# Hybrid decoder layer: two query heads take x's first k tile beside the first projection, and single-block attention products become fp32 matmuls

## The chip, the cores and the metric

The kernel runs on one core of a Trainium2 chip. The metric is device time in microseconds (us) of one launch; smaller is better. The engines are named as in the profile: PE multiplies matrices (PEld loads its weights), DVE and ACT work on vectors, POOL fills constants and issues some DMAs, SP issues most DMAs.

## What is computed

One decoder layer over 512 tokens of width 1024, all in float32:

```python
h = rms_norm(x, g_mix)
q, f, i, gate, mq, mk, mv = split(h @ W_in)      # HGRN2: 4 x 512 columns; MoBA: 3 x 512
f  = lb + (1 - lb) * sigmoid(f);  k = 1 - f;  b = cumsum over 32 tokens of log(f)
A  = causal((q * exp(b)) @ (k * exp(-b)).T)       # per head, in chunks of 32
o  = A @ i + (q * exp(b)) @ S;   S = decay * S + (k * exp(b_last - b)).T @ i
o  = rms_norm_per_head(o) * silu(gate)
m  = causal softmax attention of mq, mk (partial rotary), mv, 4 heads of 128
x  = x + concat(o, m) @ W_out
x  = x + cross_attention(rms_norm(x), mem)        # 256 memory tokens
x  = x + relu(rms_norm(x) @ W1) ** 2 @ W2         # width 4096
out = rms_norm(x)
```

With 512 tokens in two blocks of 256 and the own block always taken, the block choice of the MoBA heads is plain causal attention.

## The kernel before, in words

**Products of three.** Almost every large product is written as three fp32r matmuls: each operand is split into a rounded part (`hi`, written by ACT) and the rest (`lo`, a subtraction on DVE), and hi*hi, hi*lo and lo*hi are added in PSUM. Weights come in units of 128x1024 (512 KB): SP loads a unit into one of three raw buffers (`wr4` for unit 4), ACT writes `wh4`, DVE writes `wl4`. A raw buffer is free for the load three units on when its `wl` is written. `need(u)`, called as a stage begins to use unit u, asks for loads six units ahead and splits two ahead (`load_unit`, `split_unit`).

**Stages.** They follow each other on PE: `hf` (forget logits, units 0 to 3, all four heads side by side, k tile by k tile of x), `hi` (the recurrence's input, units 4 to 7, token-major, `tm_stage`), `hq` (queries, units 8 to 11, one head after the other, `fm_stage`), `mv`, `mkq`, `hg`, then the output projection `wo`, cross-attention, the MLP and the last norm. Each takes 24 matmuls of 128x512 for one unit. The norm's factor is not applied to x ahead of the products, but to their results: `norm_rows` sums x's squares (`nr`, two matmuls during `hf`), then `rsqrt_of` makes the root by Ln and Exp on ACT (`rb1`).

**The recurrence.** `ev_f` multiplies `hf` by the root, takes the sigmoid on ACT and the lower bound on DVE, all into `Fz`. One Ln over all four heads gives `lnf`. `hgrn_pre(h)` makes the running sums `b` (a scan on DVE), the exponentials `eb`, `kt` and `Fz` on ACT and some twenty small DVE steps (`dc`, `ee`, `pp`, `ss`, `ke`). `ev_q` takes a head's finished `hq` and writes `qx0`, `qx1` (two halves of the tokens) and `q4` on DVE. `hgrn_out(h)` transposes `ke` (`ket`), multiplies `qx` with `kt` and `Fz` on PE (`a`, 28 small matmuls), and goes on to `pd`, the state `S` and the output `ho`.

**Attention.** `moba_head` makes the scores in four blocks of queries (`sc`: block s has (s+1) times 128 keys), the softmax, transposes the probabilities (`pt`) into `PT` and their low parts into `PL` and unused corners of `PT`, and multiplies by the values `Vm`, `Vml` (`po`).

**Order.** The start, up to the last k tile of `hf`, is kept in the order in which it is written (`ordered`). From there a scheduler sets the order on each engine from the dependencies and its own costs, and the small steps of `hgrn_pre`, `hgrn_out` and `moba_head` are put between the large matmuls by `pump` when a planner (`Pace`) takes their operands to be ready. Each engine then runs its list strictly in order. Sums of later weights are made in memory by DMAs that POOL issues (`m`, `u`), on a queue of their own, in marked places of PE's list.

**Start.** SP loads x's first k tile (256 KB); ACT's own queue loads the first k tile of unit 0 in two pieces of 128 KB (heads 0 and 1, heads 2 and 3). PE meanwhile runs `warm`, products of ones that nobody reads.

Of the kernel before, what the change touches and what calls it, by code (L numbers as in the profile page):

```python
# [8 lines left out]
F32 = mybir.dt.float32  # L9
F32R = mybir.dt.float32r  # L10
# [5 lines left out]
P = 128  # L16
D = 1024
T = 512
# [107 lines left out]
def hybrid_layer(ctx: ExitStack, tc: tile.TileContext, xT, memT, ws, vecs, consts, rots, out):  # L126
# [40 lines left out]
    def acc_bank(name):  # L167
        return pacc.tile([P, T], F32, tag="acc", name=name)
# [130 lines left out]

    transfers = all_sums()  # L300
    AFTER = mybir.DependencyInfo(mybir.DependencyClass.Sync, mybir.DependencyReason.DATA)
    marks = [None]

    def more_sums():
# [25 lines left out]
            return line[u - W_WO][0] in ("wo", "xo")  # L330
        return u % 2 == 0 and (4 <= u - FF2 < 14 or u - FF2 >= 26)

    held = []

    def later(f):
        held[0].append(f) if held else f()

    def split_raw(u, raw, a, b, eng=None):
        A.activation(his[u][:, a:b], raw[:, a:b], AF.Copy)

        def lower(hi=his[u], lo=los[u]):
            (eng or V).tensor_sub(lo[:, a:b], raw[:, a:b], hi[:, a:b].bitcast(F32))
        later(lower)
# [57 lines left out]
        if s == 2:  # L401
            more_sums()

    def need(u):
        marks.append(last_mm[0])
        if MLP <= u + SPLIT_AHEAD < FF2:
            f1_prep(*divmod(u + SPLIT_AHEAD - MLP, 7))
            return
        last = MLP if u < MLP else UNITS
        most = RAWS if u < MLP else 2 * RAWS  # L410
        want_load, want_split = min(last, u + LOAD_AHEAD + 1), min(last, u + SPLIT_AHEAD + 1)
        while state["split"] < want_split or state["load"] < want_load:
            if state["load"] < want_load and state["load"] - state["split"] < most:
                load_unit()
            elif state["split"] < want_split:
                split_unit()
            else:
                break
        if MLP - 6 <= u < MLP - 2:
            for what in ("A", "B", "cC", "D")[u - MLP + 6]:  # L420
                f1_load(0, what)
        if MLP - 7 <= u < MLP - 2:
            more_sums()
# [3 lines left out]

    side = []
    made = {}
    GAP, SLACK, WARM = 4, 2.5, 11  # L430
    since = [0]
    last_mm = [None]

# [81 lines left out]
                        between(u + j)  # L515
            u += size

    def tm_stage(u0, act, ntok, evac, name):

        accs = [acc_bank(f"{name}{t}") for t in range(ntok)]  # L520
        for j in range(4):
            need(u0 + j)
            hi, lo = his[u0 + j], los[u0 + j]
            for t in range(ntok):
                for kk in range(2):
                    a_hi, a_lo = act(2 * j + kk)
                    a_hi, a_lo = a_hi[:, t * P:(t + 1) * P], a_lo[:, t * P:(t + 1) * P]
                    w_hi, w_lo = hi[:, kk * T:(kk + 1) * T], lo[:, kk * T:(kk + 1) * T]
                    st = j == 0 and kk == 0
                    mm(accs[t], a_hi, w_hi, st, False)  # L530
                    mm(accs[t], a_hi, w_lo, False, False)
                    mm(accs[t], a_lo, w_hi, False, j == 3 and kk == 1)
                if j == 3:
                    evac(t, accs[t])
# [38 lines left out]
    def split_first(v, k, h=slice(None)):  # L573
        hi, lo, raw = (by_k(t)[:, h, k] for t in (his[v], los[v], raws[v]))
        A.activation(hi, raw, AF.Copy)
        V.tensor_sub(lo, raw, hi.bitcast(F32))

    SY.dma_start(vec, vecs)
    load_x(0)
    load_first(0, 0, slice(0, 2), A)  # L580
    load_first(0, 0, slice(2, 4), A)
    load_x(1)
    load_first(0, 1)
    load_x(2)
# [56 lines left out]
    A.activation(x0h[:, :T // 2], x0r[:, :T // 2], AF.Copy, scale=gain(G_MIX, 0))  # L641
    V.scalar_tensor_tensor(x0l, x0r, gain(G_MIX, 0), x0h.bitcast(F32), op0=ALU.mult, op1=ALU.subtract)
    split_first(0, 0, slice(2, 4))
    split_x(1)
    split_first(0, 1)
    load_first(3)
# [22 lines left out]
    def rsqrt_of(dst, src, div):  # L669

        A.activation(dst, src, AF.Ln, bias=eps, scale=1.0 / div)
        A.activation(dst, dst, AF.Exp, scale=-0.5)

    def column_sums(ps, src, n, name, later=None):

# [47 lines left out]


    accs = [(acc_bank if j < 2 else side_bank)(f"hf{j}") for j in range(HEADS)]
    norm_x = norm_rows(Sx, T, rb1, rc1)
    next(norm_x)
    for k in range(KT):
        if k % 2 == 0:
            need(k // 2)  # L730
        if k == KT - 1:
            next(norm_x)
            lower_bounds()
            ordered.__exit__(None, None, None)
        a_hi, a_lo = x_act(k)
        for hs in ((0, 1), (2, 3)) if k in (0, 2) else ((0,), (1,), (2,), (3,)):
            w = {h: [by_k(t[k // 2])[:, h, k % 2] for t in (his, los)] for h in hs}
            for h in hs:
                mm(accs[h], w[h][0], a_hi, k == 0, False)
            for h in hs:  # L740
                mm(accs[h], w[h][1], a_hi, False, False)
            for h in hs:
                mm(accs[h], w[h][0], a_lo, False, k == KT - 1)
    for h in range(HEADS):
        ev_f(h, accs[h])
    start(norm_x, "nx", 1.0)
    u = 4
# [100 lines left out]
        drain("nx")  # L848
        A.activation(Vh[:, t, :], acc, AF.Copy, scale=rc1[:, t:t + 1])

    tm_stage(u, x_act, 4, ev_hi, "hi")
    u += 4

    def ev_q(h, acc):
# [17 lines left out]
                         H["pp"][:, t0:t0 + 2, :, None].to_broadcast([P, 2, 4, CHUNK]))  # L872
        start(hgrn_out(h, qx, q4), ("out", h))

    fm_stage(u, x_act, T, ev_q, "hq", ONE * 4)
    u += 4


    Vm, Vml = s8(F32R, "Vm"), s8(F32R, "Vml")

    def ev_mv(t, acc):
        A.activation(Vm[:, t, :], acc, AF.Copy, scale=rc1[:, t:t + 1])
        V.scalar_tensor_tensor(Vml[:, t, :], acc, rc1[:, t:t + 1], Vm[:, t, :].bitcast(F32), op0=ALU.mult, op1=ALU.subtract)

# [10 lines left out]
    def rope(acc, name, scale=None):  # L895

        z, sh = s2(F32, name), s2(F32, "rsh")
        V.stream_shuffle(sh[:32], acc[:32], swap)
        for to, x, t in ((z, acc, turn_z), (sh[:32], sh[:32], turn_sh)):
            if scale is None:  # L900
                V.tensor_mul(to, x, t)
            else:
                V.scalar_tensor_tensor(to, x, scale, t, op0=ALU.mult, op1=ALU.mult)
        V.tensor_add(z[:32], z[:32], sh[:32])
        hi, lo = s2(F32R, f"zh{name}"), s2(F32R, f"zl{name}")
        A.activation(hi, z, AF.Copy)
        V.tensor_sub(lo, z, hi.bitcast(F32))
        return hi, lo

    def moba_head(h, q, k):  # L910
        PT, low0 = s8(F32R, f"PT{h}"), s2(F32R, f"PL{h}")
        pn = {}

        def low(j):

            return PT[:, NT - j, :(NT - j) * P] if j else low0

        def scores(s):
            w = (s + 1) * P
            ps = side_bank("sc")  # L920
            qs = slice(s * P, (s + 1) * P)
            smm(ps[:, :w], q[0][:, qs], k[0][:, :w], True, False)
            smm(ps[:, :w], q[0][:, qs], k[1][:, :w], False, False)
            smm(ps[:, :w], q[1][:, qs], k[0][:, :w], False, True)
            un, p = s2(F32, "un"), s2(F32, "pn")
            um, ssum, rs = sm(1, "um"), sm(1, "ssum"), sm(1, "rs")
            V.tensor_tensor_reduce(out=un[:, :w], in0=ps[:, :w], in1=cmask[:, T - w:],
                                   scale=1.0, scalar=BIG, op0=ALU.add, op1=ALU.min, accum_out=um)
            A.activation(p[:, :w], un[:, :w], AF.Exp, bias=um, scale=-1.0, accum_out=ssum)
            V.reciprocal(rs, ssum)  # L930
            V.tensor_scalar(p[:, :w], p[:, :w], rs, None, op0=ALU.mult)
            pn[s] = p

        def turn(i):
            w = (i + 1) * P
            pt = side_bank("pt")
            for j in range(i + 1):
                transpose(pt[:, j * P:(j + 1) * P], pn[i][:, j * P:(j + 1) * P])
            blocks = pt[:, :w].rearrange("p (j c) -> p j c", c=P)
            hi = PT[:, :i + 1, i * P:(i + 1) * P]  # L940
            A.activation(hi, blocks, AF.Copy)
            for j in range(i + 1):
                V.tensor_sub(low(j)[:, (i - j) * P:(i - j + 1) * P], blocks[:, j], hi[:, j].bitcast(F32))
            del pn[i]

        for i in (3, 2, 1, 0):
            yield [*q, *k]
            scores(i)
        for i in (3, 2, 1, 0):
            yield [pn[i][:, :(i + 1) * P]]  # L950
            turn(i)
        yield [PT[:, 0, :], low0]
        po = side_bank("po")
        for j in range(NT):
            v_hi, v_lo = (v[:, j, h * P:(h + 1) * P] for v in (Vm, Vml))
            p_hi = PT[:, j, j * P:]
            smm(po[:, j * P:], v_hi, p_hi, j == 0, False)
            smm(po[:, j * P:], v_lo, p_hi, False, False)
            smm(po[:, j * P:], v_hi, low(j), False, j == NT - 1)
            if j == 1:  # L960
                yield [PT]
        A.activation(mixhi[1][:, h, :], po, AF.Copy)
        V.tensor_sub(mixlo[1][:, h, :], po, mixhi[1][:, h, :].bitcast(F32))

# [812 lines left out]
```

## Time and profile before

| | |
|---|---|
| time, median of 3 runs | 720.04 us (719.31 to 720.17) |
| span of the profiled execution | 717.5 us |
| PE busy | 709.5 us, 99% of the span |
| DVE, ACT, POOL busy | 580.7, 451.8, 81.1 us |
| first `hf` matmul starts | 5.57 us |
| last matmul starts | 710.43 us |
| DMA | 155.58 MB, mean 217 GB/s |

The profile gives no device time of the execution that it was taken in, only its span; the median of the three runs lies 2.5 us above that span. In the profile's rows a name is a tile (`hf<-xhi,wl` is a matmul that writes `hf` from `xhi` and `wl`), an x and a number is a count, and square brackets hold the idle time ahead of a row and what ended it. An fp32 matmul shows as two records, an fp32r matmul as one.

### The profile page before, as it was taken

To read this page: it belongs to the slowest core of one execution; us is meant where nothing else is said; L and a number is where in the kernel's file an instruction comes from. 1 tells how busy PE (TensorE), PEld (TensorE's weight loads), DVE (VectorE), ACT (ScalarE), POOL (GpSimd) and SP (SyncE) were. 2 spreads that over 40 slices of the span, in tenths; PEclk is the share of its full clock that TensorE was granted. 3 is DMA by queue.
4 is the path that set the end of the run, shared out by engine and by line. 5 is a ranking of instruction groups with operands and counts; after the bars stand their busy time and mean duration, and the time that the engine had idled before them with its cause. 6 is when DMAs were issued, how large, how long until landed. Compare 5 with 4: busy or idle time off the path is not lost.

```text
span 717.5 us, 10748 instructions
## 1 busy us (share of the span) xinstructions
PE 709.5 (99%) x4038; PEld 613.2 (85%) x4038; DVE 580.7 (81%) x882; ACT 451.8 (63%) x654; POOL 81.1 (11%) x98
## 2 busy tenths in 40 slices
PE   9999999999999999999999999999999999999996
PEld 7888888888888888888888999999999888888885
DVE  6899537898787777777578889989899999987886
ACT  7884585546586677656565865566657655546672
POOL 2511132000000000002201111011110100110000
PEclk9999999999999999999999999999999999999999
DMA  8999689975556856458986587886898965998523
GB/s 295 274 281 318 166 175 253 368 257 144 156 173 195 249 175 202 148 177 200 267 266 156 139 225 197 223 206 193 218 233 258 288 220 192 276 276 252 177 89 117
DMA packets 62531, 155.58 MB, mean 217 GB/s; under 512 B 5232, under 2 KB 19184, under 8 KB 61968
## 3 DMA queue, kind: packets, MB, share of 16 engines
q1 hardware_dynamic: 47008, 116.43, 46.3%
q0 software_dynamic: 14592, 37.75, 28.7%
q10 hardware_dynamic: 880, 0.72, 0.3%
q8 instruction: 31, 0.51, 0.3%
q14 instruction: 20, 0.16, 0.1%
HBM read 152.79 MB, written 48.23 MB: 280 GB/s over the span
## 4 chain that ended last, share of the span: by engine, by line
PE 98%; DMA 1%; ACT 0%; DVE 0%; DVEq 0%; SPq 0%; issue 0%; ACTq 0%
PE Y L118 16%; PE X L118 12%; PE xo L118 8%; PE XB L118 6%; PE XA L118 6%; PE mkq L118 6%; PE xq L118 6%; PE wo L118 6%; PE mv L118 3%; PE hg L118 3%; PE hq L118 3%; PE Z L118 3%; PE hf L118 3%; PE memX L118 3%; PE hi L118 3%; PE memY L118 2%
## 5 line engine op out<-in xcount | busy, mean ns | idle before, releaser
L118 DVE TENSOR_TENSOR wl<-wr,wh 128x1024 fp32r<-128x1024 f32 (+2 forms) x139 | 165.6, 1196 | 33.8 <-ACT wh L118 27.1
L118 ACT ACTIVATE wh<-wr 128x1024 fp32r<-128x1024 f32 (+2 forms) x139 | 142.8, 1036 | 75.0 <-PE X L118 16.3
L240 POOL DMA_DIRECT2D u<-in_ws_dram x32 | 27.4, 874 | 320.9 <-PE xt L118 87.7
L118 PE MATMUL X<-op,wh 128*128 128x512 f32 (+1 forms) x264 | 62.9, 385 | 0.0
L118 PEld LDWEIGHTS X<-op,wh 128*128 128x128 f32 x264 | 47.2, 189 | 8.5
L118 PE MATMUL Y<-op,wh 128*128 128x512 f32 x192 | 47.2, 391 | 0.0
L118 PEld LDWEIGHTS Y<-op,wh 128*128 128x128 f32 x192 | 35.0, 189 | 6.6
L118 PEld LDWEIGHTS X<-op,wl 128*128 128x128 f32 x256 | 33.5, 191 | 1.6
L118 PE MATMUL X<-op,wl 128*128 128x256 f32 x256 | 34.1, 282 | 0.0
L118 PE MATMUL Y<-OS,wh 128*128 128x256 f32 x256 | 33.4, 283 | 0.0
L118 PEld LDWEIGHTS Y<-OS,wh 128*128 128x128 f32 x256 | 32.5, 192 | 0.7
L118 DVE TENSOR_TENSOR op<-g,op 128x1024 fp32r<-128x1024 f32 x24 | 29.3, 1219 | 2.8 <-ACT op L118 2.8
L118 ACT ACTIVATE op<-g 128x1024 fp32r<-128x1024 f32 x28 | 29.3, 1045 | 0.6 <-PE XB L118 0.6
L118 ACT ACT_TABLE_LOAD x20 | 25.7, 1283 | 2.2 <-issue 1.8
L118 PEld LDWEIGHTS Y<-op,wl 128*128 128x128 f32 x192 | 25.3, 191 | 1.3
L118 PE MATMUL Y<-op,wl 128*128 128x256 f32 x192 | 25.7, 282 | 0.0
L118 PE MATMUL xq<-x1hi,wl 128*128 128x512 f32 x64 | 25.6, 399 | 0.0
L118 PE MATMUL mkq<-xhi,wh 128*128 128x512 f32 x64 | 25.4, 397 | 0.0
L118 PE MATMUL mkq<-xhi,wl 128*128 128x512 f32 x64 | 25.4, 397 | 0.0
L118 DVE TENSOR_TENSOR wl<-wD,wh 128x1024 fp32r<-128x1024 f32 x15 | 18.4, 1224 | 8.6 <-ACT wh L118 7.9
L118 PE MATMUL xq<-x1hi,wh 128*128 128x512 f32 x64 | 25.3, 396 | 0.0
L118 PE MATMUL mkq<-xlo,wh 128*128 128x512 f32 x64 | 25.2, 394 | 0.0
(370 smaller groups left out, 1914.0 us busy)
## 6 DMA issues: line engine op xcount, KB each, us to landing
wr<-in_ws_dram SPq DMA_DIRECT2D x87, 512.0 KB, 5.0
u<-in_ws_dram POOLq DMA_DIRECT2D x32, 512.0 KB, 6.8
wr<-u SPq DMA_DIRECT2D x32, 512.0 KB, 4.4
u<-in_ws_dram SPq DMA_DIRECT2D x16, 512.0 KB, 11.9
wr<-m SPq DMA_DIRECT2D x16, 512.0 KB, 3.5
m<-in_ws_dram POOLq DMA_DIRECT2D x12, 512.0 KB, 9.8
m<-in_ws_dram POOLq DMA_DIRECT2D x16, 256.0 KB, 6.0
wA<-in_ws_dram SPq DMA_DIRECT2D x8, 512.0 KB, 5.1
```

The lines of the kernel that those rows point to most:

```text
L118: return f(*args, **kw)
L240: return nc.gpsimd.dma_start(dst, src, accum_op=ALU.add, max_dma_last_dim=4 * D)
```

## The change

**At the start.** `warm` has 8 products in place of 11. The load of unit 0's first tile for heads 2 and 3 goes from ACT's queue to SP's, behind x's first tile. Behind it SP loads 128 KB more, the first k tile of the `hq` weights of heads 0 and 1 (`qr`), which ACT and DVE split into `qh` and `ql`. After the first k tile of `hf`, PE runs the six matmuls of heads 0 and 1 of `hq` for that tile; the `hq` stage itself then begins with k tile 1 for these heads. So `hq0` and `hq1` hold two accumulators (`q_accs`) from the start, and the accumulators of `hi` for tokens 0 to 255 come from the banks of the side steps (`beside`).

**Between the root and the recurrence.** The last k tile pair of `hf` asks for one split less (`SPLIT_AHEAD - 1`), and the ACT halves of the splits of units 5 and 6 are ordered behind the root's Exp (`BEHIND`, a rule for the scheduler, no wait). `ev_f` is written in the order 2, 0, 1, 3.

**In attention.** The first score block (128 queries by 128 keys) and the last block of `po` are one fp32 matmul of unsplit operands each, in place of three fp32r ones. The score block 0 comes first of its head. The unsplit probabilities `PE0` to `PE3` are copied by ACT, and the splits of the last value tile and of the last probability block fall away on DVE.

```diff
-    GAP, SLACK, WARM = 4, 2.5, 11
+    GAP, SLACK, WARM = 4, 2.5, 8
...
+        if u in (5, 6):
+            tc.add_manual_dep(rounded.ins, first_root[0].ins.name, BEHIND)
...
-    def need(u):
+    def need(u, ahead=SPLIT_AHEAD):
...
-        accs = [acc_bank(f"{name}{t}") for t in range(ntok)]
+        accs = [(side_bank if t in beside else acc_bank)(f"{name}{t}") for t in range(ntok)]
...
-    load_first(0, 0, slice(2, 4), A)
+    load_first(0, 0, slice(2, 4))
+    SY.dma_start(q_raw.rearrange("p (n c) -> p n c", n=QE), ws[W_HQ:W_HQ + QE, :, :P].rearrange("n p c -> p n c"))
...
+    A.activation(q_hi, q_raw, AF.Copy)
+    V.tensor_sub(q_lo, q_raw, q_hi.bitcast(F32))
...
-        A.activation(dst, dst, AF.Exp, scale=-0.5)
+        first_root.append(A.activation(dst, dst, AF.Exp, scale=-0.5))
...
-            need(k // 2)
+            need(k // 2, SPLIT_AHEAD - (k == KT - 2))
...
+        if k == 0:
+            cols = [slice(n * P, (n + 1) * P) for n in range(QE)]
+            for acc, c in zip(q_accs, cols):
+                mm(acc, q_hi[:, c], a_hi, True, False)
+            for acc, c in zip(q_accs, cols):
+                mm(acc, q_lo[:, c], a_hi, False, False)
+            for acc, c in zip(q_accs, cols):
+                mm(acc, q_hi[:, c], a_lo, False, False)
...
-    tm_stage(u, x_act, 4, ev_hi, "hi")
+    tm_stage(u, x_act, 4, ev_hi, "hi", beside=(0, 1))
...
-    fm_stage(u, x_act, T, ev_q, "hq", ONE * 4)
+    for n in range(QE):
+        need(u + n)
+        for k in range(1, KT):
+            fm_k(u + n, q_accs[n], x_act, k, False, k == KT - 1)
+        ev_q(n, q_accs[n])
+    fm_stage(u + QE, x_act, T, lambda n, acc: ev_q(n + QE, acc), "hq", ONE * (4 - QE))
...
+            if s == 0:
+                smm(ps[:, :w], q[2][:, qs], k[2][:, :w])
+            else:
+                smm(ps[:, :w], q[0][:, qs], k[0][:, :w], True, False)
...
+            if j == NT - 1:
+                smm(po[:, j * P:], Vlast[:, h * P:(h + 1) * P], last, False, True)
+                break
```

How this moves the rows is seen at three places. On ACT, behind the matmuls of `nr`, stood before (`rb1` is the root, `wh5` the ACT half of unit 5's split):

```order
L118 ACTIVATE nrh_251<-Sx_163 128x512
L118 ACTIVATE wh4_309<-wr4_255 128x1024
L118 ACTIVATE wh5_339<-wr5_257 128x1024
L118 ACTIVATE wh6_406<-wr6_259 128x1024
L118 ACTIVATE rb1_242<-nr_250,eps_118 128x512
L118 ACT_TABLE_LOAD
L118 ACTIVATE rb1_242<-rb1_242 128x512
L118 ACTIVATE lbv_245<-lbv_245 128x8
L118 ACT_TABLE_LOAD
L118 ACTIVATE Fz_244<-Fz_244 128x512 x4
L118 ACTIVATE wh7_461<-wr7_313 128x1024
L118 ACT_TABLE_LOAD
```

and stands now:

```order
L118 ACTIVATE wh4_320<-wr4_260 128x1024
L118 ACTIVATE rb1_245<-nr_255,eps_118 128x512
L118 ACT_TABLE_LOAD
L118 ACTIVATE rb1_245<-rb1_245 128x512
L118 ACTIVATE lbv_248<-lbv_248 128x8
L118 ACTIVATE wh5_407<-wr5_262 128x1024
L118 ACT_TABLE_LOAD
L118 ACTIVATE Fz_247<-Fz_247 128x512 x4
L118 ACTIVATE wh6_417<-wr6_264 128x1024
L118 ACTIVATE wh7_472<-wr7_324 128x1024
L118 ACT_TABLE_LOAD
L118 ACTIVATE lnf_401<-Fz_247 128x2048
```

The splits of units 5 and 6 have moved from ahead of the root to between the root and `lnf`; next on ACT, in both, is `wh8`, one `Fz`, a table load and `eb0`. On DVE, at the same place, stood before (`wl5` is the DVE half of unit 5's split, `b` the scan):

```order
L118 TENSOR_TENSOR wl4_310<-wr4_255,wh4_309 128x1024
L118 TENSOR_TENSOR wl5_340<-wr5_257,wh5_339 128x1024
L118 TENSOR_TENSOR lbv_245<-vec_112 128x4
L118 TENSOR_TENSOR wl6_407<-wr6_259,wh6_406 128x1024
L118 TENSOR_TENSOR lbv_245<-vec_112,lbv_245 128x4 x2
L118 TENSOR_TENSOR Fz_244<-hf0_246,rb1_242 128x512
```

and stands now, from the last `Fz` product of the root to the scan:

```order
L118 TENSOR_TENSOR Fz_247<-hf3_252,rb1_245 128x512
L118 TENSOR_SCALAR lbv_248<-lbv_248 128x4
L118 TENSOR_TENSOR wl5_408<-wr5_262,wh5_407 128x1024
L118 TENSOR_SCALAR Fz_247<-Fz_247,lbv_248 128x512 x4
L118 TENSOR_TENSOR wl6_418<-wr6_264,wh6_417 128x1024
L118 TENSOR_TENSOR own_441<-rb1_245,ident_121 128x512
L118 TENSOR_TENSOR wl7_473<-wr7_324,wh7_472 128x1024
L118 TENSOR_REDUCE rc1_246<-own_441 128x4
L118 SCALAR_TENSOR_TENSOR b_451<-scan_mask_116,lnf_401 128x512
```

Two subtractions of 128x1024 have moved from ahead of the root's products to behind them. Further on, where DVE takes up head 0's queries, stood before:

```order
L118 TENSOR_TENSOR ke3_691<-Fz_244,ss3_667 128x384
L118 TENSOR_TENSOR qx0_696<-hq0_641,eb0_442 128x2x128
L118 TENSOR_TENSOR wl12_754<-wr12_571,wh12_753 128x1024
L118 TENSOR_TENSOR qx0_696<-qx0_696,dc0_479 128x2x64
L118 TENSOR_TENSOR qx0_696<-qx0_696,ee0_475 128x2x32
L118 TENSOR_TENSOR q4_698<-qx0_696,pp0_476 128x256
L118 TENSOR_TENSOR qx1_697<-hq0_641,eb0_442 128x2x128
L118 TENSOR_TENSOR qx1_697<-qx1_697,dc0_479 128x2x64
L118 TENSOR_TENSOR qx1_697<-qx1_697,ee0_475 128x2x32
```

and stands now:

```order
L118 TENSOR_TENSOR wl12_757<-wr12_582,wh12_756 128x1024
L118 TENSOR_TENSOR ke3_695<-Fz_247,ss3_675 128x384
L118 TENSOR_TENSOR qx0_703<-hq0_253,eb0_453 128x2x128
L118 TENSOR_TENSOR qx0_703<-qx0_703,dc0_490 128x2x64
L118 TENSOR_TENSOR qx0_703<-qx0_703,ee0_486 128x2x32
L118 TENSOR_TENSOR q4_705<-qx0_703,pp0_487 128x256
L118 TENSOR_TENSOR qx1_704<-hq0_253,eb0_453 128x2x128
L118 TENSOR_TENSOR qx0_745<-hq1_254,eb1_466 128x2x128
L118 TENSOR_TENSOR qx1_704<-qx1_704,dc0_490 128x2x64
L118 TENSOR_TENSOR qx1_704<-qx1_704,ee0_486 128x2x32
```

Here `wl12` has moved ahead of the first `qx0`, and one product of head 1 (`qx0_745`) has come in ahead of the last steps of head 0.

More of the change, by code (lines that the diff above doesn't have):

```diff
@@ L301, in hybrid_layer @@
     AFTER = mybir.DependencyInfo(mybir.DependencyClass.Sync, mybir.DependencyReason.DATA)
+    BEHIND = mybir.DependencyInfo(mybir.DependencyClass.NoSync, mybir.DependencyReason.SCHED_ONLY)
     marks = [None]
@@ L331, in sums_after @@
         return u % 2 == 0 and (4 <= u - FF2 < 14 or u - FF2 >= 26)
-    held = []
+    held, first_root = [], []
     def later(f):
@@ L338, in split_raw @@
     def split_raw(u, raw, a, b, eng=None):
-        A.activation(his[u][:, a:b], raw[:, a:b], AF.Copy)
+        rounded = A.activation(his[u][:, a:b], raw[:, a:b], AF.Copy)
+        if u in (5, 6):
+            tc.add_manual_dep(rounded.ins, first_root[0].ins.name, BEHIND)
         def lower(hi=his[u], lo=los[u]):
@@ L410, in need @@
         most = RAWS if u < MLP else 2 * RAWS
-        want_load, want_split = min(last, u + LOAD_AHEAD + 1), min(last, u + SPLIT_AHEAD + 1)
+        want_load, want_split = min(last, u + LOAD_AHEAD + 1), min(last, u + ahead + 1)
         while state["split"] < want_split or state["load"] < want_load:
@@ L516, in fm_stage, with tm_stage @@
             u += size
-    def tm_stage(u0, act, ntok, evac, name):
-        accs = [acc_bank(f"{name}{t}") for t in range(ntok)]
+    def tm_stage(u0, act, ntok, evac, name, beside=()):
+        accs = [(side_bank if t in beside else acc_bank)(f"{name}{t}") for t in range(ntok)]
         for j in range(4):
@@ L576, in split_first @@
         V.tensor_sub(lo, raw, hi.bitcast(F32))
+    W_HQ, QE = 8, 2
+    q_raw, q_hi, q_lo = (s2(d, n)[:, :QE * P] for d, n in ((F32, "qr"), (F32R, "qh"), (F32R, "ql")))
     SY.dma_start(vec, vecs)
@@ L725, in hybrid_layer @@
     accs = [(acc_bank if j < 2 else side_bank)(f"hf{j}") for j in range(HEADS)]
+    q_accs = [acc_bank(f"hq{j}") for j in range(QE)]
     norm_x = norm_rows(Sx, T, rb1, rc1)
@@ L743, in hybrid_layer @@
                 mm(accs[h], w[h][0], a_lo, False, k == KT - 1)
-    for h in range(HEADS):
+        if k == 0:
[6 more added lines that the diff above has]
+                mm(acc, q_hi[:, c], a_lo, False, False)
+    for h in (2, 0, 1, 3):
         ev_f(h, accs[h])
@@ L873, in ev_q @@
         start(hgrn_out(h, qx, q4), ("out", h))
-    fm_stage(u, x_act, T, ev_q, "hq", ONE * 4)
+    assert u == W_HQ
+    for n in range(QE):
[4 more added lines that the diff above has]
+    fm_stage(u + QE, x_act, T, lambda n, acc: ev_q(n + QE, acc), "hq", ONE * (4 - QE))
     u += 4
     Vm, Vml = s8(F32R, "Vm"), s8(F32R, "Vml")
+    Vlast = s2(F32, "Vlast")
     def ev_mv(t, acc):
+        if t == NT - 1:
+            A.activation(Vlast, acc, AF.Copy, scale=rc1[:, t:t + 1])
+            return
         A.activation(Vm[:, t, :], acc, AF.Copy, scale=rc1[:, t:t + 1])
@@ L907, in rope @@
         V.tensor_sub(lo, z, hi.bitcast(F32))
-        return hi, lo
+        return hi, lo, z
     def moba_head(h, q, k):
         PT, low0 = s8(F32R, f"PT{h}"), s2(F32R, f"PL{h}")
+        last = s2(F32, f"PE{h}")[:, :P]
         pn = {}
@@ L921, in scores @@
             qs = slice(s * P, (s + 1) * P)
-            smm(ps[:, :w], q[0][:, qs], k[0][:, :w], True, False)
-            smm(ps[:, :w], q[0][:, qs], k[1][:, :w], False, False)
-            smm(ps[:, :w], q[1][:, qs], k[0][:, :w], False, True)
+            if s == 0:
+                smm(ps[:, :w], q[2][:, qs], k[2][:, :w])
+            else:
+                smm(ps[:, :w], q[0][:, qs], k[0][:, :w], True, False)
+                smm(ps[:, :w], q[0][:, qs], k[1][:, :w], False, False)
+                smm(ps[:, :w], q[1][:, qs], k[0][:, :w], False, True)
             un, p = s2(F32, "un"), s2(F32, "pn")
@@ L938, in turn @@
                 transpose(pt[:, j * P:(j + 1) * P], pn[i][:, j * P:(j + 1) * P])
-            blocks = pt[:, :w].rearrange("p (j c) -> p j c", c=P)
-            hi = PT[:, :i + 1, i * P:(i + 1) * P]
+            n = min(i + 1, NT - 1)
+            blocks = pt[:, :n * P].rearrange("p (j c) -> p j c", c=P)
+            hi = PT[:, :n, i * P:(i + 1) * P]
             A.activation(hi, blocks, AF.Copy)
-            for j in range(i + 1):
+            if i == NT - 1:
+                A.activation(last, pt[:, n * P:], AF.Copy)
+            for j in range(n):
                 V.tensor_sub(low(j)[:, (i - j) * P:(i - j + 1) * P], blocks[:, j], hi[:, j].bitcast(F32))
             del pn[i]
-        for i in (3, 2, 1, 0):
+        yield [q[2], k[2]]
+        scores(0)
+        for i in (3, 2, 1):
             yield [*q, *k]
@@ L958, in moba_head @@
             smm(po[:, j * P:], v_lo, p_hi, False, False)
-            smm(po[:, j * P:], v_hi, low(j), False, j == NT - 1)
+            smm(po[:, j * P:], v_hi, low(j), False, False)
             if j == 1:
-                yield [PT]
+                yield [PT, last]
         A.activation(mixhi[1][:, h, :], po, AF.Copy)
```

## The prediction

> **What bounds the kernel now.** I read the page's chain that ended last first, then the stretch from the first real matmul to the last, by engine (in a stretch's row: its bounds, its length, and busy time and count of PE, PEld, DVE, ACT, POOL).
>
> ```profile
> PE 98%; DMA 1%; ACT 0%; DVE 0%; DVEq 0%; SPq 0%; issue 0%; ACTq 0%
> 5.57:710.50 704.93, 704.91 (x4015) 608.98 (x4016) 577.58 (x876) 448.13 (x646) 76.30 (x80) 1.00 0.76 217
> ```
>
> From 5.57 to 710.50 us PE does not stand still once. So the time falls only by what PE starts earlier or has less to do, and every wait that the change brings to PE is paid in full: PE never has idle time in which to make it good. The median of the runs, 720.04, lies 2.5 us above the profiled span of 717.5; I add differences to the median.
>
> **Start.** The timeline of PE and ACT, the DMA part of the first 1.5 us (size, us from issue to landing), and two stretches:
>
> ```profile
> 0.99 4.29 PE L118 MATMUL warm<-ones 128*128 128x128 f32 x22 [0.99 <-POOL eps L592]
> 5.01 0.51 ACT L118 ACTIVATE xhi<-xraw,vec 128x256 fp32r<-128x256 f32 x1 [1.31 <-DMA xraw<-in_xT_dram]
> 5.57 0.73 PE L118 MATMUL hf<-xhi,wh 128*128 128x512 f32 x2 [0.29 <-ACT xhi L118]
> wr<-in_ws_dram ACTq DMA_DIRECT2D x2, 128.0 KB, 3.6
> xraw<-in_xT_dram SPq DMA_DIRECT2D x1, 256.0 KB, 3.7
> 0.99:4.30 3.31, 3.31 (x15) 3.31 (x16) 0.43 (x1) 1.90 (x3) 2.96 (x10) 1.00 0.69 169
> 4.30:5.57 1.27, 0.98 (x9) 0.79 (x7) 0.37 (x2) 0.51 (x1) 0.00 (x0) 1.00 1.00 327
> ```
>
> `hf` begins when ACT has rounded half of x's first tile, and ACT waits for that tile. Its 256 KB share the DMA engines with 2 times 128 KB on ACT's queue. One of these 128 KB now goes behind it: at the 327 GB/s of the last stretch 0.40 us. The gain lies between 0 (if x0 was slow for another reason) and 0.8 (at 169 GB/s); I take 0.40. Eight `warm` products are 16 records of 3.31/15 = 0.22 us, ending at 4.5, ahead of `hf` at 5.2; they cost nothing.
>
> The six early `hq` matmuls are only moved. Their pitch is read from the end of `hf`, with the second of the two `nr` matmuls that the root waits for:
>
> ```profile
> 25.01 0.40 PE L118 MATMUL nr<-nrl,ones_r 128*128 128x512 f32 x1
> 27.79 0.39 PE L118 MATMUL hf<-xlo,wh 128*128 128x512 f32 x1
> 28.02 0.39 PE L118 MATMUL hi<-wh,xhi 128*128 128x512 f32 x1
> ```
>
> 6 x 0.23 = 1.38 us more lie ahead of `nr`, less 0.40: `nr` ends 0.98 later, at 25.01 + 0.40 + 0.98 = 26.39. They give x's second tile 1.38 us more, which covers the 0.4 us of 128 KB more on SP's queue. At head 0's `a`, further on, the same matmuls stand ahead of it as before: there PE would be 0.40 early.
>
> **Products in fp32.** A trio of 128x128 `sc` stands between two `mkq` matmuls; six records of `pd` are three fp32 products of the same size:
>
> ```profile
> 133.06 0.22 PE L118 MATMUL sc<-zhz,zhz 128*128 128x128 f32 x1
> 133.34 0.45 PE L118 MATMUL mkq<-xlo,wh 128*128 128x512 f32 x1
> 133.63 0.39 PE L118 MATMUL mkq<-xhi,wl 128*128 128x512 f32 x1
> 84.34 0.83 PE L118 MATMUL pd<-Vh,kets 128*128 128x128 f32 x6
> 84.93 0.48 PE L118 MATMUL mv<-wl,xhi 128*128 128x512 f32 x1
> 85.24 0.39 PE L118 MATMUL mv<-wh,xlo 128*128 128x512 f32 x1
> ```
>
> The trio with one large matmul takes 133.63 - 133.06 = 0.57, less 0.23 it is 0.34. Three fp32 products take 85.24 - 84.34 - 0.23 = 0.67, 0.22 each. 0.12 less per trio, 4 heads, 2 trios: **-0.97 us**, on PE, so in full. DVE loses some subtractions and ACT gains four copies, in a part where neither holds PE.
>
> **The splits behind the root.** This is the part that decides. ACT and DVE between the root and the recurrence, and DVE at head 0's queries:
>
> ```profile
> 22.98 3.03 ACT L118 ACTIVATE wh<-wr 128x1024 fp32r<-128x1024 f32 x3
> 25.91 0.67 ACT L118 ACTIVATE rb<-nr,eps 128x512 f32<-128x512 f32 x1
> 29.94 2.20 ACT L118 ACTIVATE Fz<-Fz 128x512 f32<-128x512 f32 x4
> 32.91 1.06 ACT L118 ACTIVATE wh<-wr 128x1024 fp32r<-128x1024 f32 x1 [0.78 <-DMA wr<-in_ws_dram]
> 33.99 1.28 ACT L118 ACT_TABLE_LOAD   x1
> 35.29 1.92 ACT L118 ACTIVATE lnf<-Fz 128x2048 f32<-128x2048 f32 x1
> 37.11 1.04 ACT L118 ACTIVATE wh<-wr 128x1024 fp32r<-128x1024 f32 x1
> ...
> 24.06 2.36 DVE L118 TENSOR_TENSOR wl<-wr,wh 128x1024 fp32r<-128x1024 f32 x2 [0.26 <-ACT wh L118]
> 31.17 0.16 DVE L118 TENSOR_SCALAR lbv<-lbv 128x4 f32<-128x4 f32 x1
> 61.40 0.42 DVE L118 TENSOR_TENSOR qx<-hq,eb 128x256 f32<-128x256 f32 x1
> 61.73 1.21 DVE L118 TENSOR_TENSOR wl<-wr,wh 128x1024 fp32r<-128x1024 f32 x1
> 64.20 0.22 DVE L118 TENSOR_TENSOR qx<-qx,ee 128x64 f32<-128x64 f32 x1
> 38.00:61.00 23.00, 23.00 (x103) 19.06 (x102) 22.74 (x72) 16.74 (x27) 5.95 (x8) 1.00 1.01 305
> ```
>
> Before, the root's Ln started at 25.91, straight behind three splits. Now it waits for `nr` alone and starts at 26.4, 0.5 later. From Ln to the sigmoids it is 4.03, plus unit 5's split, (25.91 - 22.98)/3 = 0.98: 31.4. Four sigmoids 2.2, the splits of units 6 and 7 1.96 (unit 7 no longer waits for its load), the table 1.30: `lnf` starts at 36.86, **1.57 later**.
>
> The second effect is larger. Unit 8's load takes unit 5's raw buffer, so it is issued when `wl5` is written. SP's waits, its rows (25.31 is unit 7, the next is unit 8) and landings of such loads (the four issued from 24 to 45, the one of 27.5 to 28, and the page's median):
>
> ```profile
> SPq L118 <- DVE wl L118: 16.0, 4, 6.0
> 26.45 0.33 SPq L118 DMA_DIRECT2D wr<-in_ws_dram  x1
> wr<-in_ws_dram SPq DMA_DIRECT2D x4, 512.0 KB, 7.7
> wr<-in_ws_dram SPq DMA_DIRECT2D x1, 512.0 KB, 9.5
> wr<-in_ws_dram SPq DMA_DIRECT2D x87, 512.0 KB, 5.0
> q0 software_dynamic: 107, 0.20, 109.2%
> ```
>
> `wl5` used to end at 24.06 + 2.36 = 26.42; now it stands behind the last `lbv` step: 31.17 + 0.07 + 0.5, plus 1.21 = 32.95. Unit 8's load is issued there, 6.5 us later, while POOL's sums fill the DMA engines (107 packets of q0 take all of the engines' time from 35 to 36). With the 7.7 of the loads of that stretch it lands at 40.65. Its split stands on ACT next after `lnf`, in a slot at 37.11 + 1.57 = 38.68, and `eb0`, which DVE needs for all that follows, stands behind it. So the split starts at 40.65 where it started at 37.11: the chain is **3.54 late**.
>
> DVE cannot catch up: it is busy for 22.74 of the 23.00 us from 38 to 61. Moving `wl12` ahead of `qx0` changes nothing in the sum; head 1's product inside adds 0.33 (61.40 to 61.73). Head 0's last `qx` step, done at 64.42 before, is done at 64.42 + 3.54 + 0.33 = 68.3. PE at that place:
>
> ```profile
> 65.39 0.32 PE L118 MATMUL a<-qx,kt 128*32 128x32 f32 x5
> 66.20 0.30 PE L118 MATMUL a<-qx,Fz 128*32 128x64 f32 x5
> 66.43 0.50 PE L118 MATMUL hq<-xlo,wh 128*128 128x512 f32 x1
> ```
>
> From the last small group to the next large matmul it is 0.23, so that matmul starts at 68.53, 2.10 later than before. Without the wait it would start at 66.03; PE stalls 2.5 us at `a` of head 0, and the 0.40 of the start is lost in it. Waiting behind `a` are all later matmuls, and units 9 and 10, issued as late behind `wl6` and `wl7`, are wanted after that wait. Sum: +2.10 - 0.97 = **+1.13, 721.2 us**.
>
> **Rivals.** *The load lands in time.* Unit 8 now has fewer loads beside it; with the page's 5.0 it lands at 37.95, ahead of its slot. Then the lag is 1.57, the last `qx` step ends at 66.32, the matmul starts at 66.55: +0.12 - 0.97 = -0.85, 719.2. A landing of 9.5, on the other side, makes the lag 5.34 and the time 723.0. The Trainium skill, "DMA: Bandwidth & Descriptors", section "Queues, rings and completion order", has each DMA engine go round robin between its queues packet by packet, which would let unit 8 begin beside the sums; by that rule this rival holds. The four loads of 7.7 in the same stretch speak against it.
>
> *No stall.* If the lag at `qx` were under 66.03 - 0.23 - 64.42 - 0.33 = 1.05 us, PE would not wait: -0.40 - 0.97 = -1.37, 718.7, and a start gain of 0.8 makes it 718.3. It ends on the faster side if `lnf` comes no more than 1.05 late and unit 8 by 38.2. ACT's list speaks against: two splits more behind the root, 1.96, against 0.78 of idle time there.
>
> *A cold clock.* 15 `warm` records took 3.31 us, 0.22 each, and the last seven, from 4.30 to 5.28, 0.14. Eight products end 0.2 after 4.30; if it comes later, as it may from run to run, `hf` runs at half rate for up to 1.7 us (half of 3.4). `nr`, the splits and unit 8's load would all be late by it: 722.9. The Trainium skill, "TensorE: Matmul & The Clock Gate", section "Part 1: The HAM clock gate", has the clock rise after one busy window of about 3.4 us that runs free of the kernel's start; 3.5 us of `warm` would cover a whole window only by luck, and by that rule this rival is the likelier. The trace had the rise 3.31 us after the first product, inside these eight.
>
> **How the numbers follow.** About 0.2% (1.44 us) is what a measurement of this kernel can tell from no change: 718.6 to 721.5. The stall with a landing near 7.7: 0.54, which ends above 721.5 when the landing takes over 8.0 us, a little under half. Load in time: 0.18, all within. No stall: 0.18, counted as faster, though its time stands at the bound. Cold clock: 0.1, slower. So faster 0.18, same 0.28 + 0.18 = 0.46, slower 0.26 + 0.1 = 0.36. The range goes from no stall (718.6) to the landing of 9.5 and the cold clock (723.0); for the likeliest case alone it is 720.0 to 722.3.
>
> **What would show it.** In the profile of the changed kernel: the first `hf` at about 5.2; `lnf` near 36.9; idle time on ACT ahead of a `wh` for a DMA near 40; a PE stall of 1 to 3.5 us ahead of `a` at 65 to 69, put down to DVE `qx`; `sc` and `po` of 128x128 as two records. No PE idle time at `a` would make it wrong, or idle time on PE at `hi` for `wl5`, or a second stall at the later heads.

## The result, and the profile after

The changed kernel takes 730.12 us (median, 728.59 to 731.49) against 719.67 (719.24 to 720.17): 1.0146 of the time before, 95% interval 1.0132 to 1.016. The forecast was 721.2 with a range that ended at 723.0. The place and the kind of the loss were forecast; its size was not, and the load that causes it is another. All figures here and below are of undisturbed executions; one of 779.31 us, at a granted clock of 0.849, and one of 1830.8 us are left out as slow.

Who waited for whom between 20 and 80 us of the changed kernel (waited for: us in total, times, longest):

```profile
POOL m L269 <- PE hf L118: 19.5, 1, 19.5
...
ACT wh L118 <- DMA wr<-in_ws_dram: 12.0, 3, 8.0
...
PE a L118 <- DVE qx L118: 8.2, 1, 8.2
DVE Fz L118 <- ACT lnf L118: 6.8, 1, 6.8
```

PE stands still for 8.2 us at `a` of head 0, where it did not wait before. The rows around it give the reason: DVE waited for ACT's `lnf`, and ACT for a load. The chain that ended last, from 51 to 75 us, has them in order of time (its rows `issue` are left out):

```profile
51.35 17.63 DMA wr<-in_ws_dram
...
69.09 1.06 ACT wh L118
70.14 0.53 ACT lnf L118
70.69 0.04 DVE Fz L118
71.30 1.22 DVE wl L118
72.52 0.47 DVE ke L118
72.99 0.34 DVE qx L118
73.38 1.79 PE a L118 x22
```

The load is that of unit 12, issued at 51.35 and landed 17.6 us later; the one that the prediction went by, unit 8's, landed in time. On ACT its split `wh12` stands ahead of head 3's exponential (`lnf`); on DVE `Fz`, `wl12` and `ke3` stand ahead of the first `qx`. PE's timeline at that place:

```profile
73.38 0.65 PE L118 MATMUL a<-qx,kt 128*32 128x32 f32 x8 [8.17 <-DVE qx L118]
75.60 0.52 PE L118 MATMUL a<-qx,Fz 128*32 128x64 f32 x6
76.06 0.80 PE L118 MATMUL hq<-xlo,wh 128*128 128x512 f32 x1
76.65 0.63 PE L118 MATMUL hq<-xhi,wl 128*128 128x512 f32 x1
```

From the first `a` to the next large matmul it was 65.39 to 66.43, 1.04 us; now it is 2.68. The stretches show why (the eighth number is the granted clock of PE):

```profile
66.00:72.00 6.00, 0.00 (x0) 0.00 (x0) 1.31 (x2) 2.90 (x4) 0.00 (x0) 0.60 0.34 136
72.00:78.00 6.00, 4.62 (x63) 3.35 (x64) 5.97 (x19) 0.05 (x1) 0.00 (x0) 0.55 0.72 232
78.00:84.00 6.00, 6.00 (x86) 5.13 (x86) 5.26 (x14) 1.66 (x3) 0.00 (x0) 1.00 0.85 289
```

In the stall the clock falls, and it stays down for about 4 us of the work behind it: the large matmuls of 76.06 to 77.47 follow each other at 0.39 to 0.59 us, where 0.23 is usual. That agrees with the Trainium skill, "TensorE: Matmul & The Clock Gate", section "Part 1: The HAM clock gate", where an idle window of about 3.4 us brings the half rate.

By places, the profiled spans differ by 728.4 - 717.5 = 10.9 us: `ket`, the row ahead of `a`, starts 0.25 earlier (64.72 for 64.97); from there to the last `a` of all heads 10.5 are lost; the attention takes 0.64 less; a side step of cross-attention makes PE wait and costs 0.6; and the tail after the last matmul is 0.65 longer.

Why is the load late? POOL's first rows, before and after:

```profile
17.09 3.21 POOL L269 DMA_DIRECT2D m<-in_ws_dram  x4 [12.93 <-PE hf L118]
22.50 2.94 POOL L269 DMA_DIRECT2D m<-in_ws_dram  x4 [2.20 <-PE hf L118]
28.49 2.40 POOL L240 DMA_DIRECT2D m<-in_ws_dram  x2 [3.04 <-PE hf L118]
```

```profile
23.64 6.12 POOL L269 DMA_DIRECT2D m<-in_ws_dram  x8 [19.50 <-PE hf L118]
33.27 2.40 POOL L240 DMA_DIRECT2D m<-in_ws_dram  x2 [3.51 <-DMA m<-in_ws_dram]
```

The first copies of POOL's sums are issued 6.5 us later. `need`, asked for one split less at the last pair of `hf`, also takes up unit 8's load one call later, because a load may be only three units ahead of the splits; and the sums are tied to that load and wait for the mark set one call before it. DMA shows it (the last two numbers are its share and GB/s), before and after:

```profile
22.00:28.00 6.00, 6.00 (x27) 4.90 (x27) 4.81 (x8) 5.53 (x7) 2.94 (x4) 1.00 0.87 272
46.00:52.00 6.00, 6.00 (x28) 4.99 (x27) 6.00 (x9) 2.45 (x5) 1.76 (x3) 1.00 0.97 309
```

```profile
22.00:28.00 6.00, 6.00 (x28) 4.89 (x27) 3.61 (x7) 3.00 (x4) 4.36 (x6) 1.00 0.44 139
46.00:52.00 6.00, 6.00 (x28) 4.97 (x27) 6.00 (x12) 3.63 (x6) 0.65 (x1) 1.00 1.10 264
```

From 22 to 28 us the DMA engines are half idle, and what was left undone comes back later, at a time when they are full but move less. So there are two candidate causes: these late sums, and the late raw buffers of units 5 and 6 that the prediction went by.

### The profile page after: what moved, and what is told of

It is laid out like the page before. It is cut to its first block, busy times and chain, and to the rows that moved or that the text cites. A ratio compares the mean times of both kernels' runs of the same rounds, so it can differ in the third digit from the quotient of the medians.

```text
span 728.4 us, 10723 instructions
## 1 busy us (share of the span) xinstructions
PE 711.4 (98%) x4024; PEld 613.2 (84%) x4024; DVE 579.7 (80%) x878; ACT 452.1 (62%) x659; POOL 81.0 (11%) x98
## 4 chain that ended last, share of the span: by engine, by line
PE 90%; DMA 5%; DVE 2%; ACT 1%; issue 1%; DVEq 0%; SPq 0%; ACTq 0%
PE Y L118 16%; PE X L118 12%; PE xo L118 7%; PE XB L118 6%; PE XA L118 6%; PE xq L118 6%; PE mkq L118 6%; PE wo L118 6%; DMA wr<-in_ws_dram 5%; PE mv L118 3%; PE hg L118 3%; PE Z L118 3%; PE hf L118 3%; PE memX L118 3%; PE memY L118 2%; PE xs L118 1%
## 5 line engine op out<-in xcount | busy, mean ns | idle before, releaser
L118 PE MATMUL xq<-x1lo,wh 128*128 128x512 f32 x64 | 25.2, 393 | 0.0
## 6 DMA issues: line engine op xcount, KB each, us to landing
m<-in_ws_dram POOLq DMA_DIRECT2D x12, 512.0 KB, 10.9
```

What stands on the lines that cost most here:

```text
L118: return f(*args, **kw)
```

## The experiments

In each, the difference to the kernel named is all that was changed. "Before" is 719.5 to 719.7 us in every comparison.

**Without the ordering rule** (both parts that belong to it taken out of the changed kernel).

```diff
-        if u in (5, 6):
-            tc.add_manual_dep(rounded.ins, first_root[0].ins.name, BEHIND)
...
-            need(k // 2, SPLIT_AHEAD - (k == KT - 2))
+            need(k // 2)
```

> The changed kernel without the ordering rule (the splits of units 5 and 6 go ahead of the root again, the full split-ahead is asked for). Theory A, late buffers: the rule alone delays unit 5's and 6's low parts and with them the loads of units 8 to 10, and the 8.2 us stall at a of head 0 comes from there; without it no stall above 0.3 us, and 718.4 to 719.2 us, the gains of the start and of the fp32 products. Rival B, the start: 128 KB more and six matmuls ahead of nr shift the later loads against POOL's sums by themselves; then the stall stays above 4 us and the time above 724.

720.59 us, 1.0011 of before (1.0002 to 1.002). No wait at `a`; unit 12's load took 7.1 us. The loss of 10 us hangs on these two parts, the rule and the one split less; rival B is out. But the gains do not come out either: 0.9 us slower than before, not 0.5 to 1.3 faster.

**The rule alone** (both parts added to the kernel before).

> The kernel before with the ordering rule alone (and one split less asked for at the last pair of hf). Here ACT's list keeps lnf of head 3 ahead of the split of unit 12. Theory A in its DMA form: unit 12's load lands late (over 12 us) and the stall at a is there though the order of those two is the old one; 724 to 730 us. Rival C, ACT's order: the late load hurts only since the split of unit 12 has come ahead of head 3's exponential; then here only the lag of 1.5 us shows and the time is 719.5 to 722.

723.84 us, 1.0064 (1.0043 to 1.0085). Unit 12's load is issued at 50.1 and lands 15.0 us later, though `lnf` stands ahead of its split here. PE waits 2.3 us at `a`, and from `ket` to the last `a` it loses 3.3 us. So the late load comes with the rule and the one split less, without the rest of the change; rival C is out, and the time is just below theory A's range. The trace is one of the three shorter of the six executions (722.2 to 722.5 us; the others took 725.2 to 727.1). Beside the rest of the change the load lands 3.8 us later still, and then the clock falls too, which it did not after 2.3 us.

**Two causes apart.** The changed kernel with the sums on time, and, on the other side, without the rule but with one split less asked for:

```diff
-    def more_sums():
+    def more_sums(back=-2):
...
-            more_sums()
+            more_sums(-3 if u == 8 else -2)
```

> The changed kernel with one line more: POOL's first four sum copies (m0_0) wait for the mark one k tile pair earlier, as they did before; the ordering rule and all else stay. Theory D, late sums: with one split less asked for at the last pair of hf, unit 8's load and with it POOL's first sums are taken up one mark later (23.6 for 17.1 us), the DMA engines stand half idle from 22 to 28 us, and the backlog makes unit 12's load land at 69; with the sums on time it lands by 60 and the stall at a is under 2.5 us: 719.5 to 722.5 us. Theory A, late raw buffers: loads 8 to 10 stay 6 to 9 us late, unit 12 still lands after 65, and the time is 726 or more.

```diff
-        if u in (5, 6):
-            tc.add_manual_dep(rounded.ins, first_root[0].ins.name, BEHIND)
```

> The changed kernel without the ordering rule, but with one split less asked for at the last pair of hf. The splits of units 5 and 6 stand ahead of the root, so their raw buffers come free as before; POOL's first sums still wait for the later mark. Theory D: the DMA engines are half idle from 22 to 28 us, unit 12 lands after 62, PE stalls at a: 722 to 727 us. Theory A: no stall, 719.5 to 721.

725.01 (1.0064, 1.0043 to 1.0085) and 726.36 us (1.0083, 1.0056 to 1.0111). The waits of PE, and the DMA rows of the load of unit 12 (issued at 53.70 and at 50.22), first with the sums on time, then with the buffers on time:

```profile
PE a L118 <- DVE qx L118: 4.7, 1, 4.7
22.00:28.00 6.00, 6.00 (x28) 4.92 (x27) 4.10 (x8) 2.94 (x4) 2.94 (x4) 1.00 0.91 290
wr<-in_ws_dram SPq DMA_DIRECT2D x1, 512.0 KB, 11.9
```

```profile
PE a L118 <- DVE qx L118: 5.2, 1, 5.2
22.00:28.00 6.00, 6.00 (x28) 4.92 (x27) 4.95 (x9) 4.48 (x6) 4.73 (x7) 1.00 0.52 169
wr<-in_ws_dram SPq DMA_DIRECT2D x1, 512.0 KB, 17.4
```

Neither theory holds alone: each cause by itself brings a stall of 5 us in its trace and 5 to 7 us of median time, and the two together 10. These traces are of long executions, 727.36 and 726.92 us; the shortest of each kernel took 722.4 and 722.1, and how long PE stood still there is not known. The first kernel has the step that the prediction went by: unit 8's load, issued at 33.2, landed 7.8 us later at 41.0, and ACT waited 2.2 us for it. But its stall, too, goes by way of unit 12: issued 4.0 us later than in the kernel before, that load took 11.9 us, and DVE waited 2.8 us for the `lnf` behind it. By these rows some 1.9 of the 4.7 us are the prediction's own step (an estimate, 4.7 - 2.8).

**The order on ACT.** Unit 12's split behind head 3's exponential:

```diff
+        if u == 12:
+            tc.add_manual_dep(rounded.ins, last_exp[3].ins.name, BEHIND)
```

> The changed kernel with the ACT split of unit 12 ordered behind head 3's exponential (lnf), as it stood before; the loads stay late. DVE then has qx0's first product ahead of wl12 and the rest behind it, so PE still waits for a load that lands near 69: theory of the load alone, the stall stays above 6 us and the time above 727. Rival C, ACT's order: the 6.8 us for which DVE waited for lnf are saved in good part, the stall shrinks to 3 to 5 us, and the time is 723 to 727.

729.82 us, 1.0143 (1.0129 to 1.0157), not to be told from the changed kernel. `wl12`, which waits for the same load, then stands between the first and the second step of `qx`. PE waited 5.6 us in two parts in place of 8.2, but in this profiled execution its `hf` had also ended 2.3 us later; what the order is worth is left open. Rival C's saving of 3 us or more is out, for the four executions took 728.9 to 730.6 us.

**Contention.** The additions of the sums, and what follows them (copies that SP issues on its own queue, then copies by POOL), go eight units later, in the changed kernel and in the version with the sums' first copies on time:

```diff
-            return 2 * (u >= 8) + (u >= 22)
+            return 2 * (u in (8, 9)) + 4 * (18 <= u < 26) + 2 * (u >= 26) + (u >= 22)
```

> The changed kernel, with POOL's sums from the first additions on (from unit 10's to unit 17's place) moved eight units on, to where no load is wanted soon; the first copies stay late, the ordering rule stays. Theory E, contention: the loads of units 8 to 13 take 7 to 18 us because 2 KB packets of the sums share the DMA engines with them; without the sums they land within 6 us of their issue, the chain on ACT and DVE is late by the splits alone (1.6 us), PE waits 0 to 1.5 us at a: 719.3 to 721. Rival A, late issue alone: unit 12's load is issued at 51 or later whatever shares the engines, and the stall stays above 4 us: 724 or more.

> The same with the first copies on time as well (the version with the sums on time, its additions moved eight units on). Only the late raw buffers are left of the two causes. Theory E: as above or a little better, 719 to 720.5, no stall above 1.5 us at a. Rival A: the stall of the version with the sums on time (4.7 us) stays, 724 to 726.

722.65 (1.0041, 1.0025 to 1.0057) and 722.18 us (1.004, 1.0025 to 1.0055): less than rival A allows, more than theory E's 721 and 720.5. In both, the wait at `a` and the load of unit 12, issued at 51.5, read

```profile
PE a L118 <- DVE qx L118: 0.2, 1, 0.2
wr<-in_ws_dram SPq DMA_DIRECT2D x1, 512.0 KB, 3.3
```

The issue is as late as in the changed kernel, the buffers are as late, ACT's order is the same, and 17.6 us have become 3.3. The stall goes from 8.2 to 0.2 us (0.8 to 0.9 lost from `ket` to the last `a`). So the loads are late because of the DMAs of the sums. Which of them does it is not separated, for the edit moves three kinds at once, and for unit 12 the changed kernel's trace points at SP's own copies:

```profile
49.16 0.62 SPq L237 DMA_DIRECT2D m<-in_ws_dram  x1
m<-in_ws_dram SPq DMA_DIRECT2D x1, 512.0 KB, 18.0
51.35 0.33 SPq L118 DMA_DIRECT2D wr<-in_ws_dram  x1
wr<-in_ws_dram SPq DMA_DIRECT2D x1, 512.0 KB, 17.6
```

The copy stands ahead of the load in SP's queue and landed at 67.2, the load 1.8 us behind it, at 69.0. In the kernel before, the same copy was issued at 47.45 and took 7.6 us, and the load landed 2.6 us behind it, at 57.7. In each of the eleven kernels in which this copy stands ahead of it, the load landed 1.2 to 2.6 us behind the copy; with the sums moved, no copy stands there. So most of the 17.6 us is time in which the copy ahead had not landed. That the copy in turn is slowed by POOL's additions, the last of which land at 57 in place of 49, fits the rows but was not tested by itself. How much the additions take is seen in the kernel before, POOL's queue from 34 to 40 us (packets, MB, share of the engines' time):

```profile
q0 software_dynamic: 579, 1.12, 102.2%
```

All of the engines' time goes into 1.12 MB. At that point the loads of units 8 and 9 were over there, or nearly; in the changed kernel the loads of units 8 to 13 are all issued while additions run. The time does not come back to that of before: PE loses 1.5 us between 205 and 215 us, in `wo`, about half of it in waits for ACT and DVE. No trace of a kernel with the sums in place has this loss, so it comes with the moved sums; I had not expected it.

**The parts of the gain.** The fp32 products alone on the kernel before:

> The kernel before with the fp32 products of attention alone. By the price of pd, 0.12 us less for each of eight trios: -0.97, 718.7 us. By what the two traces show between mv and wo, -0.64: 719.0 us. A rival that fp32 costs as much as three fp32r products: 719.7, no change.

720.61 us, 1.0012 (1.0003 to 1.0021): slower, against all three. In the trace they do save 0.64 us between `mv` and `wo`. Against it stand 0.7 us in the tail, and in the profiled execution 1.3 us lost in `hf`, 0.8 of them in waits for weights that this change does not touch.

The changed kernel without the rule, with 11 and with 10 warm products, and the start alone with 10:

> The changed kernel without the ordering rule and with 11 warm products in place of 8. They end at 5.28, so hf begins at about 5.3 in place of 4.9, but at the full rate. If eight products left the clock low, as the trace of the changed kernel has it (two hf matmuls at 0.47 us), the two versions end within 0.3 us of each other; if the clock rises by itself at 4.3, this one is 0.4 us slower than the version with 8.

719.62 us, 0.9998 (0.999 to 1.0007): no change from before, and 1.0 us less than with 8 products, where the expectation had them within 0.3 of each other. The executions overlap (718.8 to 721.1 and 719.5 to 721.9), and at `ket` the two traces differ by 0.2 only; the rest is not explained.

> The start alone: early hq matmuls, moved load, banks and ev_f's order, without the ordering rule and with products in three in attention, and 10 warm products so that the clock is up when hf begins. hf should begin at 4.9 to 5.1 at the full rate, 0.45 to 0.65 earlier than before; if all of it reaches the end, 719.1 us; if the loads of hf's next tiles eat it, as in the two versions without the rule (0.1 early at ket), 719.6; small waits behind 270 us, as these two had, would make it 720.

720.45 us, 1.0013 (1.0004 to 1.0021). In the trace `ket` starts 0.42 us earlier, and the tail is 0.6 longer.

> The best of the parts: the changed kernel without the ordering rule and with 10 warm products. hf begins at 4.8 to 5.0 at the full rate. From the parts: -0.42 at ket, -0.64 by the fp32 products, +0.65 in the tail: 719.2 us against 719.65; small waits behind 270 us, as two of the versions without the rule had, would make it 719.6 to 720.5.

721.03 us, 1.0017 (1.0009 to 1.0026), with runs from 719.03 to 722.75: above both times of the expectation. No version beats the kernel before. PE's first rows of the last two, the start alone first:

```profile
0.99 4.08 PE L118 MATMUL warm<-ones 128*128 128x128 f32 x20 [0.99 <-POOL eps L596]
4.83 0.71 PE L118 MATMUL hf<-xhi,wh 128*128 128x512 f32 x2
5.38 0.63 PE L118 MATMUL hf<-xhi,wl 128*128 128x512 f32 x2
```

```profile
0.99 4.63 PE L118 MATMUL warm<-ones 128*128 128x128 f32 x20 [0.99 <-POOL eps L596]
5.28 1.20 PE L118 MATMUL hf<-xhi,wh 128*128 128x512 f32 x2
6.28 0.61 PE L118 MATMUL hf<-xhi,wl 128*128 128x512 f32 x1
```

The same ten products end at 5.07 in one execution and at 5.62 in the other; there the first two `hf` matmuls take 1.00 us in place of 0.55, about half the rate. I take this for a clock that rises later, from the times alone: the granted clock reads 1.00 for this stretch in both profiles. So the point from which PE runs at the full rate moves between executions, as the Trainium skill, "TensorE: Matmul & The Clock Gate", section "Part 1: The HAM clock gate", says, and 8 or 10 products do not always reach it: in the version without the rule but with one split less, eight did nearly, with 0.62 us for the first two `hf` matmuls. Eleven took 4.73 us in the version with the fp32 products alone and 4.29 in the kernel before.

## Why the prediction was wrong, point by point

**The load that lands late.** The step that failed is "With the 7.7 of the loads of that stretch it lands at 40.65". In the changed kernel unit 8's load, issued at 33.15 (forecast: 32.95), took 4.8 us, landed at 38.0, ahead of its slot, and ACT did not wait for it. `lnf` started at 36.97 (36.86). To this point the rival "the load lands in time" was right; whether by a round robin between the queues, no run shows. But the working ended there. The sentence "units 9 and 10, issued as late behind `wl6` and `wl7`, are wanted after that wait" priced only issue times, as if a late load cost no other load anything. The backlog went on for 30 us and came out at unit 12: 17.6 us for a load, where the rows ahead of the prediction had 9.5 at most. And "Moving `wl12` ahead of `qx0` changes nothing in the sum" took `wl12` as 1.2 us of DVE's work; it is also a wait for unit 12's load, on either side of the first `qx`, as the experiment on ACT's order shows. So the stall that was forecast as 2.5 us, from one late load, was 8.2, from another.

**POOL's queue.** The rows of POOL stood in the same order as before, and the prediction put them at nothing, without a reason. Their waits had changed: the first eight copies had two marks ahead of them before and one after. This alone brings 5.2 us of stall in the trace of the version that keeps only the one split less, and no term of the sum holds it.

**The place.** "A PE stall of 1 to 3.5 us ahead of `a` at 65 to 69, put down to DVE `qx`": the place and the releaser are right, the size was 8.2.

**The clock.** "Eight `warm` products ... cost nothing" was wrong: the first two `hf` matmuls took 0.94 us at 4.92 to 5.86, and the gain of the start, 0.65 us at the first `hf`, was 0.25 at `ket`. The rival "a cold clock" was the case by these times, at 0.4 us, not 1.7. That the stall lowers the clock again, so that waiting costs more than the wait, was not thought of; from `ket` to the last `a` 10.5 us were lost with 8.2 us of idle time. Not all of the 2.3 us between is the clock: with the rule alone 3.3 us were lost with 2.3 us of idle time, at a clock of 1.00.

**The fp32 products.** -0.97 was forecast, -0.64 measured. A `sc` block went as priced; in the changed kernel it is

```profile
137.61 0.38 PE L118 MATMUL sc<-z,z 128*128 128x128 f32 x2
137.74 0.48 PE L118 MATMUL mkq<-xlo,wh 128*128 128x512 f32 x1
138.06 0.40 PE L118 MATMUL mkq<-xhi,wl 128*128 128x512 f32 x1
```

138.06 - 137.61 - 0.23 = 0.22, against 0.34 for the trio. The last block of `po` saves nearly as much. From the start of its group to the second large matmul behind it, in the kernel before and in the changed one:

```profile
179.19 0.28 PE L118 MATMUL po<-PT,Vm 128*128 128x256 f32 x1
180.10 0.40 PE L118 MATMUL hg<-xhi,wl 128*128 128x512 f32 x1
```

```profile
188.52 0.28 PE L118 MATMUL po<-PT,Vm 128*128 128x256 f32 x1
189.32 0.39 PE L118 MATMUL hg<-xlo,wh 128*128 128x512 f32 x1
```

That is 0.91 and 0.80 us, 0.11 less. So the price of a trio was right, to about 0.9 us for all eight; some 0.3 us of it is lost again in the matmuls around them, whose order has changed. The prediction had no term for that, and what makes it is open.

**The chances.** Slower had 0.36 and the range ended at 723.0. All rivals were taken one at a time; in the kernel two of them held, the cold clock and the load in time with its lag (1.57 us forecast, 1.68 measured at `lnf`), and neither was the main cause. That PE stalls at `a` at all was right for the wrong load: with unit 8 in time and no later load held up, the prediction's own sum has 719.2 us.

## What to carry to other kernels

When a split or a load is moved, write down for each DMA queue what it carries in each stretch before and after, not only when the moved load is issued: here a stretch in which the DMA engines stood half idle was paid for 30 us later, by a load that had not been moved and that stood behind copies in its own queue. A list in the same order can still be a different list; compare the waits too, on the queues that nobody looks at above all. On an engine that is 99% busy a stall can cost more than it lasts: those of 4.7, 5.2 and 8.2 us, in which the clock fell, lost 7.1, 7.0 and 10.5 us from `ket` to the last `a`; that of 2.3 us, in which it did not, lost 3.3.

## What the runs showed of the hardware

A load of 512 KB took 3.3 us with the engines to itself (unit 12 with the sums moved), and 7 to 18 us with DMAs of the sums beside it and ahead of it (7.1 for unit 12 without the rule, 17.6 in the changed kernel). The load of unit 8, issued at 33.2 in both, landed in 4.8 us in the changed kernel, where the first copies still ran, and in 7.8 with the sums on time, where the additions did.

The results' last DMAs take longer in all versions but one. Issues of the last 8 us, kernel before and changed kernel:

```profile
out_dram<-g SPq DMA_DIRECT2D x4, 256.0 KB, 2.5
```

```profile
out_dram<-g SPq DMA_DIRECT2D x4, 256.0 KB, 3.0
```

The version with the rule alone, which adds no tile to the memory on the chip, has 2.5 as well; the other eleven, which all add tiles, have a tail behind the last matmul that is 0.6 to 0.7 us longer. The cause is open; it takes back as much as the fp32 products save.
